# Both tiles' delta rule ahead of the norms, output rows tile by tile, and filling products in front of two norms

## The chip, the cores and the metric

The kernel runs on one core of a Trainium2 chip. The metric is the device time of one execution in microseconds, as the median of the runs.

## What is computed

Two blocks of a network run one after the other on 256 rows of width 1024, batch 1. The first is a mixer of sparse attention, pooling and a gated spatial unit, then attention to a memory, then a convolutional FFN. The second is a mixer of a gated delta rule, an indexed sparse attention and a long convolution, then cross attention to a second memory (`mem_2`), then an MLP. Each part adds its result to the rows `x` of the residual stream. What the change touches, cut from the reference:

```
x = x + rms_norm(memory_attention(h, m, w_mq, w_mk, w_mv, w_mo), mem_norm_post)
h = rms_norm(x, ffn_norm_pre)
x = x + rms_norm(conv_ffn(h, w_up, conv_w, conv_b, w_down), ffn_norm_post)
...
gamma = where(tril, exp(where(tril, decay_i - decay_j, 0)), 0)
a_mat = where(strict, (k beta) k^T * gamma, 0);  solve (I + a_mat) [u, w] = [v beta, k beta exp(decay)]
step: v_new = u - w S;  o = q exp(dec) S + (q k^T gamma) v_new
      S = S exp(last) + (k exp(last - dec))^T v_new
o = rms_norm_2(o, norm_g) * silu(z)
```

All of it is in fp32, to be matched closely.

## The kernel before

The 256 rows are two tiles of 128. A product of fp32 numbers is made of three passes of TensorE (`mm3`, L240): each operand is split in a high and a low part, and high x high, low x high and high x low are summed in PSUM. `load_w` (L213) brings a weight tile of 128 x 1024 by a DMA on SP's queue into one of four `wr` buffers; ScalarE copies it to `wh` (the high part), VectorE subtracts in two halves to make `wl`. After `give(share)` every so many tiles are subtracted on GpSimd in one piece instead (L238).

The program is written as Python generators, and the emission order with the dependences sets the order on each engine; a tile framework places the waits. `lead(main, fill, ratio)` emits `ratio` steps of a filling generator for each step of a main one, and `beside` mixes two.

Four places matter here.

- **`block1_mem` (L960)**, the memory attention. `out(n, qs, i)` adds output products of `w_mo` for half n, weight quarters qs and row tile i. At its end it loads and norms `mem_2` (`mem_T`, L343) into `m2T`, loads the last constants and three quarters of the key half of `xa_wkv`, adds the last output products and calls `residual` (L448): for tile 0, then tile 1, squares (ScalarE), scaling (L461), the power -1/2 (`rms_pow`, L293, on GpSimd, L298), and the sum into x (L467).
- **`ffn` (L1043)** begins with `norm_T` (L322): for each tile the squares, the power and the scaled rows `xh` (L340), then four 128 x 128 transposes on TensorE for each half (L317), which ScalarE (L307) and VectorE (L308) copy to high and low parts `hl`. Behind it stands `xa_k` (L1641), the key half of the second memory (48 products of 512 columns, made of m2T and `xa_wkv`), whose products TensorE takes as filling. `block2_mix` (L1170) begins in the same way with `norm_T` and the value half, `xa_v`.
- **`gdn_decay` (L1253)** makes the decay mask `gamma`: outer differences (L1289), a minimum with 0 (L1293), an exponential (L1294) and a multiplication with the upper triangle on GpSimd (L1295). The lengths of q and k follow, whose power -1/2 is `gdr_y` on GpSimd (L260). The keys `ds_kn` of the sparse attention (L1524, transposed at L1525) stand behind in VectorE's queue.
- **`gdn` (L1388)** runs the two tiles in turn. For a tile: state products (L1402, L1404, tile 1 only), the solution w (L1412), the new state (L1418, tile 0 only), the output (L1423) on VectorE (L1426 to L1429), then its norm: squares, the power `gdo_y` on GpSimd, the gate z (L1440, L1441), transposes (L1444) and their copies (L1447, L1448) into the first half of `mixT`. Filling beside it is `fill2`: the end of the sparse attention, the norm of the long convolution (`conv_norm`, L1615: statistics, `sg_v` at L1632, transposes at L1623 and L1636), the residual rows added to the banks of the output sum (`add_x`, L1229), and the products of `w_out_2` with the mixer's second half (stage 0, L406 to L408). After that come the products with the first half (stage 1).

Of the kernel before, what the change touches and what calls it, by code (L numbers as in the profile page):

```python
# [8 lines left out]
F32 = mybir.dt.float32  # L9
# [11 lines left out]
P = 128  # L21
# [25 lines left out]
_CONST = [("ident", 128), ("blk8", 8), ("blk2", 2), ("upper", 128), ("trineg", 128), ("lev", 7 * 128)]  # L47
# [79 lines left out]
class Net:  # L127
# [202 lines left out]
    def row_norm_T(self, x, g, dst, i, tag="tp"):  # L330

        nc = self.nc
        ss = self.half_sums(EPS)
# [3 lines left out]
        for n in range(2):  # L337
            sl = slice(n * 512, (n + 1) * 512)
            a = self.t([P, 512], "xh", bufs=4)
            nc.vector.scalar_tensor_tensor(a, x[:, sl], r, g[:, sl], op0=ALU.mult, op1=ALU.mult)  # L340
            self.transpose_split(a, dst, i, 4 * n, 4, tag)

    def mem_T(self, name, gname, place=None, tag="fl"):  # L343

        nc = self.nc
        g = self.grow(gname)
# [16 lines left out]
    def proj_half(self, wname, n, h, nk=NCH, tag="cc", late=False, ws=()):  # L363
# [14 lines left out]
        return a  # L378

# [68 lines left out]
    def residual(self, xs, acc, gname=None):  # L448

        nc = self.nc  # L450
        g = self.grow(gname) if gname else None
        for i in range(2):
            x = xs[i]
            if gname:
                ss = self.half_sums()
                z = []
                for n in range(2):
                    sl = slice(n * 512, (n + 1) * 512)
                    self.square_sum(acc[n][i], ss[:, n:n + 1])
                    a = self.t([P, 512], "xh", bufs=4)  # L460
                    nc.vector.scalar_tensor_tensor(a, acc[n][i], ROOT_D, g[:, sl], op0=ALU.mult, op1=ALU.mult)  # L461
                    z.append(a)
                r = self.rms_pow(ss)
            for n in range(2):
                sl = slice(n * 512, (n + 1) * 512)
                if gname:
                    nc.vector.scalar_tensor_tensor(x[:, sl], z[n], r, x[:, sl], op0=ALU.mult, op1=ALU.add)  # L467
                else:
                    nc.vector.tensor_tensor(x[:, sl], acc[n][i], x[:, sl], op=ALU.add)
        return xs  # L470

# [333 lines left out]
    def fill1(self, hT, mixT, x2):  # L805
# [9 lines left out]
        mT = self.mem_T("mem", "mem_norm_kv", "t3")  # L815
# [144 lines left out]
    def block1_mem(self, x):  # L960
# [47 lines left out]
        query(1)  # L1008
        step(first)
# [886 lines left out]
```

## Time and profile before

| | |
|---|---|
| median of three runs | 862.19 us (858.83, 862.19, 863.39) |
| the profiled execution | 860.27 us, span 858.5 us |
| mean granted clock of TensorE | 0.987 |
| TensorE busy | 829.3 us (97%) |
| VectorE, ScalarE, GpSimd busy | 623.6, 494.6, 71.0 us |

One execution was profiled. Its span runs from the first to the last instruction; 1.8 us lie around it. The busy time of TensorE counts overlapped products, so 97% says that it nearly always has something under way, and the places of interest are the few microseconds in which it has not, and the ones in which it runs at a lower granted clock (a column of the stretches).

### The profile page before, as it was taken

The page shows a single profiled execution, that of the slowest core. Times are in us where ns is not written, and L with a number is a line of the kernel's source. Part 1 is how long each engine was busy: PE and PEld are TensorE (multiplying, and loading weights), DVE is VectorE, ACT ScalarE, POOL GpSimd, SP SyncE. Part 2 cuts the span into 40 slices and gives each one's busy share as a digit, 9 for nine tenths or more (in the row PEclk, how much of TensorE's full clock was granted, in tenths as well). Part 3 has the DMA queues.
Part 4 walks back from the last instruction along what each step waited for, and adds up shares of the span by engine and source line. Part 5 has one row for each costly group of instructions (what it writes and reads, how often), then busy time and mean ns, then how long its engine had stood idle before and what let it go on. Part 6 is the DMA issues. An engine that isn't in the chain of part 4 may idle for free.

```text
span 858.5 us, 13849 instructions
## 1 busy us (share of the span) xinstructions
PE 829.3 (97%) x5117; PEld 729.5 (85%) x5117; DVE 623.6 (73%) x1394; ACT 494.6 (58%) x889; POOL 71.0 (8%) x105
## 2 busy tenths in 40 slices
PE   8899999999998999999999999999899999999998
PEld 6898877889877888888887998989798988888886
DVE  5469765554577988988886797988676876666663
ACT  6256554554665776766665764656365665555552
POOL 1224101121110000000001002000100000000000
PEclk9899999999999999999999999999999999999999
DMA  8994323464562576665642562302153366655651
GB/s 267 287 291 161 99 78 117 145 226 148 171 222 98 196 233 213 218 212 183 194 150 74 195 194 80 98 1 81 36 179 99 106 214 195 188 182 195 192 182 68
DMA packets 41007, 138.86 MB, mean 162 GB/s; under 512 B 4851, under 2 KB 6292, under 8 KB 40940
## 3 DMA queue, kind: packets, MB, share of 16 engines
q1 hardware_dynamic: 37440, 130.49, 46.6%
q10 hardware_dynamic: 2988, 6.06, 2.1%
q0 software_dynamic: 512, 1.44, 1.0%
q8 instruction: 40, 0.66, 0.3%
q14 instruction: 27, 0.22, 0.1%
HBM read 136.00 MB, written 1.44 MB: 160 GB/s over the span
## 4 chain that ended last, share of the span: by engine, by line
PE 76%; DVE 8%; DMA 7%; ACT 3%; issue 2%; POOL 2%; ACTq 0%; SPq 0%; POOLq 0%; DVEq 0%
PE tp L527 14%; PE tp L528 8%; PE fl L242 6%; PE fl L244 6%; PE fl L243 6%; PE cc L242 4%; PE cc L244 4%; PE cc L243 4%; DMA wr<-in_w_in_dram 3%; PE tp L530 2%; PE tp L242 2%; DVE wl L232 2%; PE tp L243 2%; PE tp L244 2%; PE cc L787 1%
## 5 line engine op out<-in xcount | busy, mean ns | idle before, releaser
L232 DVE TENSOR_TENSOR wl<-wr,wh 128x512 fp32r<-128x512 f32 (+2 forms) x446 | 296.8, 690 | 93.4 <-ACT wh L230 92.8
L230 ACT ACTIVATE wh<-wr 128x1024 fp32r<-128x1024 f32 (+2 forms) x223 | 231.8, 1042 | 101.0 <-PE fl L243 25.0
L527 PE MATMUL tp<-hl,wh 128*128 128x512 f32 x532 | 190.6, 397 | 0.0
L528 PE MATMUL tp<-hl,wl 128*128 128x256 f32 x608 | 158.2, 281 | 0.0
L528 PEld LDWEIGHTS tp<-hl,wl 128*128 128x128 f32 x608 | 114.7, 189 | 6.6
L527 PEld LDWEIGHTS tp<-hl,wh 128*128 128x128 f32 x532 | 100.0, 188 | 21.6
L242 PE MATMUL tp<-hl,wh 128*128 128x256 f32 x176 | 51.4, 293 | 3.5 <-ACT wh L230 3.5
L244 PE MATMUL tp<-hl,wl 128*128 128x256 f32 x176 | 51.1, 290 | 0.0
L243 PE MATMUL tp<-hl,wh 128*128 128x256 f32 x176 | 50.9, 290 | 0.0
L1062 DVE SCALAR_TENSOR_TENSOR ff_y<-ff_u,col,ff_y 128x255 f32<-128x255 f32 x88 | 41.9, 478 | 1.4 <-ACT ff_y L1060 1.2
L242 PE MATMUL fl<-hl,wh 128*128 128x256 f32 x144 | 42.1, 292 | 0.4 <-ACT sg_v L893 0.4
L242 PE MATMUL cc<-wh,ff_h 128*128 128x512 f32 x108 | 42.4, 393 | 0.0
L242 PE MATMUL fl<-wh,ff_h 128*128 128x512 f32 x108 | 42.3, 392 | 0.0
L243 PE MATMUL cc<-wl,ff_h 128*128 128x512 f32 x108 | 42.3, 392 | 0.0
L244 PE MATMUL fl<-wh,ff_h 128*128 128x512 f32 x108 | 42.3, 392 | 0.0
L244 PE MATMUL cc<-wh,ff_h 128*128 128x512 f32 x108 | 42.3, 392 | 0.0
L243 PE MATMUL fl<-wl,ff_h 128*128 128x512 f32 x108 | 42.0, 389 | 0.0
L237 ACT ACTIVATE ff_h<-ff_y 128x256 fp32r<-128x256 f32 x54 | 22.3, 416 | 33.7 <-PE fl L244 25.2
L243 PE MATMUL fl<-hl,wh 128*128 128x256 f32 x144 | 41.7, 289 | 0.0
L244 PE MATMUL fl<-hl,wl 128*128 128x256 f32 x144 | 41.6, 289 | 0.0
L242 PEld LDWEIGHTS tp<-hl,wh 128*128 128x128 f32 x176 | 35.0, 199 | 3.9 <-ACT wh L230 3.7
L531 ACT ACTIVATE ff_y<-tp 128x256 f32<-128x256 f32 x32 | 12.3, 383 | 43.8 <-PE tp L530 43.8
(504 smaller groups left out, 1952.4 us busy)
## 6 DMA issues: line engine op xcount, KB each, us to landing
wr<-in_mlp_w_dram SPq DMA_DIRECT2D x64, 512.0 KB, 3.5
wr<-in_w_up_dram SPq DMA_DIRECT2D x44, 512.0 KB, 3.7
wr<-in_w_in_dram SPq DMA_DIRECT2D x31, 512.0 KB, 4.3
wr<-in_w_down_dram SPq DMA_DIRECT2D x22, 512.0 KB, 3.4
wr<-in_w_out_dram SPq DMA_DIRECT2D x16, 512.0 KB, 3.6
grow<-in_rows_dram ACTq DMA_DIRECT2D x8, 512.0 KB, 5.2
wr<-in_w_mk_dram SPq DMA_DIRECT2D x8, 512.0 KB, 4.5
wr<-in_w_mv_dram SPq DMA_DIRECT2D x8, 512.0 KB, 3.5
```

Source lines behind the costliest of these rows:

```text
L230: nc.scalar.activation(hi, raw, AF.Copy)
L232: nc.vector.tensor_tensor(lo[:, q], raw[:, q], hi[:, q].bitcast(F32), op=ALU.subtract)
L237: nc.scalar.activation(hi, raw, AF.Copy)
L242: nc.tensor.matmul(out, a[0], b[0], start=first, stop=False)
L243: nc.tensor.matmul(out, a[0], b[1], start=False, stop=False)
L244: nc.tensor.matmul(out, a[1], b[0], start=False, stop=last)
L527: nc.tensor.matmul(pts[e], hi, both[:, :, k, :], start=k == 0, stop=False)
L528: nc.tensor.matmul(pts[e][:, :S], lo, h[0][:, k, :], start=False, stop=False)
L530: nc.tensor.matmul(pts[e], hi, both[:, :, k, :], start=False, stop=True)
L531: nc.scalar.activation(dst[:, e, :], pts[e][:, S:], AF.Copy)
L787: nc.tensor.matmul(out[:, h * 64:(h + 1) * 64], pT[:, (e * (i + 1) + b) * P:(e * (i + 1) + b + 1) * P], vsw[b][:, vo:vo + 64], start=(b == ...
L1062: nc.vector.scalar_tensor_tensor(y[:, e, k:], a[:, :S - k], self.c("conv_w", 44 * (2 - k) + c), y[:, e, k:], op0=ALU.mult, op1=ALU.add)
```

## The change

Four things are changed; the results stay the same sums.

- In `block1_mem`, `give(0)` stands behind the second query, so that no weight tile from there is subtracted on GpSimd. The two rows tiles of `mem_2` are loaded and normed ahead of the last two quarters of both output halves, and both rows of gains are loaded there. The output products of tile 0 (both halves) come first, then tile 0's part of the residual (`residual_tile`), the second memory's transposes, and then tile 1's products and residual.
- `norm_beside` puts three of the four weight quarters of the key half (`ffn`) and of the value half (`block2_mix`) in front of the norm, and the fourth behind it. `half_steps` is the generator of the quarters; `row_norm_T` is cut in `row_norm` and `rows_T`.
- In `gdn_decay` the minimum and the mask are one operation, with a constant of large negative numbers below the diagonal (`neglow`, 128 more columns of constants); the multiplication on GpSimd is left out.
- In `gdn` a first loop runs both tiles' recurrence, and a second loop both norms, with one more `yield` between a norm and its transposes.

```
@@ block1_mem
         query(1)
+        self.give(0)
         step(first)
...
-        for i in range(2):
-            out(0, (2, 3), i)
-        self.m2T = self.mem_T("mem_2", "norm_mem_2", tag="tp")
+        g2, g = [self.grow(n) for n in ("norm_mem_2", "mem_norm_post")]
+        self.m2T = self.new_T()
+        rows = [self.wp.tile([P, D], F32, tag="wr", name=self.nm("wr")) for _ in range(2)]
+        for i in range(2):
+            nc.sync.dma_start(rows[i], self.i["mem_2"][i])
+        m = self.row_norm(rows[0], g2)
+        out(0, (2, 3), 0)
+        self.rows_T(m, self.m2T, 0)
+        m = self.row_norm(rows[1], g2)
+        out(1, (2, 3), 0)
+        self.residual_tile(x[0], [a[0] for a in acc], g)
+        self.rows_T(m, self.m2T, 1)
...
-        for i in range(2):
-            out(1, (2, 3), i)
-        return self.residual(x, acc, "mem_norm_post")
+        for n in range(2):
+            out(n, (2, 3), 1)
+        self.residual_tile(x[1], [a[1] for a in acc], g)
+        return x
@@ ffn (block2_mix in the same way, with the value half)
-        hT = self.norm_T(x, "ffn_norm_pre")
-        self.xa_k()
+        acc, steps = self.half_steps("xa_wkv", 0, self.m2T, ws=self.ahead)
+        hT = self.norm_beside(x, "ffn_norm_pre", steps)
+        self.xa_k(acc)
@@ new
+    def half_steps(self, wname, n, h, tag="cc", ws=()):
+        a = [self.ps(tag) for _ in range(2)]
+        def steps():
+            for q in range(NCH // 2):
+                w = ws[q] if q < len(ws) else self.load_w(self.i[wname][n, q])
+                for i in range(2):
+                    self.part_N(a[i], h, w, i, q, NCH)
+                yield
+        return a, steps()
+    def norm_beside(self, x, gname, steps):
+        for _ in range(3):
+            next(steps)
+        hT = self.norm_T(x, gname)
+        for _ in steps:
+            pass
+        return hT
@@ gdn_decay
+        low4 = self.con[:, CON["neglow"]:CON["neglow"] + P].unsqueeze(1).to_broadcast([P, H, P])
...
-            nc.vector.tensor_scalar(gam[:, i], gam[:, i], 0.0, None, op0=ALU.min)
+            nc.vector.scalar_tensor_tensor(gam[:, i], gam[:, i], 0.0, low4, op0=ALU.min, op1=ALU.add)
             nc.scalar.activation(gam[:, i], gam[:, i], AF.Exp)
-            nc.gpsimd.tensor_tensor(gam[:, i], gam[:, i], up4, op=ALU.mult)
@@ gdn, behind the recurrence of a tile
             yield
 
+        for i in range(2):
+            tsl = slice(i * P, (i + 1) * P)
+            o = os[:, i]
             sv = self.t([P, H], "gd_sv")
...
             nc.vector.tensor_tensor(o, o, b4(ro), op=ALU.mult)
+            yield
             pt = self.ps()
```

On SP's queue the two loads of `mem_2` move from behind the sixth tile of `w_mo` to behind the fourth. At three places TensorE's order shows the change.

The first is the norm ahead of the FFN. Before, the groups of transposes of `xh` (L317) stand among the last products of the key half (`cc`, of m2T's `hl`), starting behind its first quarters:

```order
1278 L244 MATMUL cc_2805<-t_557_2659,hl_2594 128x512
1279 L317 MATMUL tp_2761<-con,xh_2759 128x128 x4
1280 L242 MATMUL cc_2805<-t_557_2659,hl_2594 128x512
1281 L317 MATMUL tp_2770<-con,xh_2768 128x128 x4
1282 L243 MATMUL cc_2805<-gd_rhs_2658,hl_2594 128x512
1283 L244 MATMUL cc_2805<-t_557_2659,hl_2594 128x512
1284 L317 MATMUL tp_2789<-con,xh_2787 128x128 x4
```

In the changed kernel they stand together behind the third quarter, and the fourth quarter (of `wh` and `wl`) follows:

```order
1287 L244 MATMUL cc_2750<-t_571_2693,hl_2560 128x512
1288 L317 MATMUL tp_2804<-con,xh_2800 128x128 x4
1289 L317 MATMUL tp_2811<-con,xh_2802 128x128 x4
1290 L317 MATMUL tp_2832<-con,xh_2828 128x128 x4
1291 L317 MATMUL tp_2839<-con,xh_2830 128x128 x4
1292 L242 MATMUL cc_2749<-wh_2848,hl_2560 128x512
```

So all four groups moved behind 36 products, and 12 products are left behind them.

The second is the end of tile 0's delta rule. Before, behind tile 0's output (L1423) come a few filling products, tile 0's transposes for its norm (L1444), and only then tile 1's state products (L1402):

```order
2982 L407 MATMUL cc_6590<-hl_4945,wh_6669 128x256
2983 L408 MATMUL cc_6590<-hl_4945,wl_6670 128x256
2984 L1444 MATMUL tp_6528<-con,t_1060_5471 128x128 x4
2985 L1402 MATMUL tp_6609<-gd_st_6499,kq_5160 128x128 x2
2986 L1636 MATMUL fl_6581<-con,sg_v_6579 128x128
```

In the changed kernel, whose line numbers are 46 to 52 higher here, the state products (L1450, L1452) follow the output (L1471) of tile 0 at once:

```order
2968 L1466 MATMUL tp_6495<-t_1060_5474,gd_kd_6369 128x128 x4
2969 L1471 MATMUL tp_6502<-t_1060_5474,bq_1106_5658 128x128 x4
2970 L1450 MATMUL tp_6516<-gd_st_6500,kq_5163 128x128 x4
2971 L1452 MATMUL tp_6517<-gd_st_6500,kq_5163 128x128 x4
2972 L1688 MATMUL fl_6568<-con,sg_v_6566 128x128
```

Tile 0's transposes moved behind tile 1's output, 19 rows further on.

The third is tile 1's transposes. Before, they stand among the products of stage 0 of `w_out_2`:

```order
3051 L407 MATMUL fl_6591<-hl_4945,wh_6720 128x256
3052 L408 MATMUL fl_6591<-hl_4945,wl_6721 128x256
3053 L1444 MATMUL tp_6711<-con,t_1060_5471 128x128 x4
3054 L406 MATMUL fl_6591<-hl_4945,wh_6720 128x256
3055 L407 MATMUL fl_6591<-hl_4945,wh_6720 128x256
```

In the changed kernel they stand behind the last of them; the next four products are one of each bank of stage 1, and the rest of stage 1 follows:

```order
3082 L440 MATMUL fl_6600<-hl_4948,wl_6733 128x256
3083 L1496 MATMUL tp_6774<-con,t_1060_5474 128x128 x4
3084 L438 MATMUL cc_6597<-hl_4948,wh_6788 128x256
3085 L438 MATMUL cc_6598<-hl_4948,wh_6825 128x256
3086 L438 MATMUL fl_6599<-hl_4948,wh_6862 128x256
3087 L438 MATMUL fl_6600<-hl_4948,wh_6899 128x256
3088 L439 MATMUL cc_6597<-hl_4948,wh_6788 128x256
```

The products of stage 0 that stood behind these transposes moved ahead of them.

## Rows read from the trace of the kernel before

**Rows 1.** TensorE's waits over the whole run: us in total, times, longest us.
```profile
PE tp L317 <- DVE xh L340: 5.9, 4, 2.7
```

**Rows 2.** Stretches of 10 us: length, busy of five engines, clock, DMA share, GB/s.
```profile
260.00:270.00 10.00, 10.00 (x48) 8.35 (x48) 5.07 (x9) 4.73 (x13) 0.60 (x2) 0.84 0.29 108
...
460.00:470.00 10.00, 9.73 (x55) 7.87 (x54) 4.84 (x10) 4.43 (x8) 0.60 (x1) 1.00 0.29 102
...
520.00:530.00 10.00, 8.17 (x66) 7.68 (x65) 6.90 (x24) 5.17 (x14) 3.54 (x4) 0.98 0.30 105
530.00:540.00 10.00, 10.00 (x72) 9.62 (x71) 7.93 (x28) 4.81 (x8) 1.46 (x1) 0.85 0.01 2
...
600.00:610.00 10.00, 6.91 (x49) 6.24 (x48) 5.49 (x13) 3.73 (x11) 1.90 (x3) 0.90 0.16 52
610.00:620.00 10.00, 10.00 (x80) 9.82 (x79) 6.42 (x12) 4.29 (x9) 1.24 (x1) 0.93 0.01 2
```

**Rows 3.** Timeline of TensorE, 249.5 to 268.5, and VectorE's `xa_kn`: start, length, then names.
```profile
249.95 0.39 PE L242 MATMUL cc<-t,hl 128*128 128x512 f32 x1
250.17 0.39 PE L243 MATMUL cc<-bq,hl 128*128 128x512 f32 x1
...
259.80 1.04 PE L317 MATMUL tp<-con,xh 128*128 128x128 f32 x4 [2.67 <-DVE xh L340]
260.49 0.78 PE L242 MATMUL cc<-t,hl 128*128 128x512 f32 x1
...
265.79 0.63 PE L317 MATMUL tp<-con,xh 128*128 128x128 f32 x4
266.17 0.48 PE L243 MATMUL cc<-wl,hl 128*128 128x512 f32 x1
...
268.10 0.39 PE L527 MATMUL tp<-hl,wh 128*128 128x512 f32 x1
...
272.42 0.69 DVE L1654 TENSOR_TENSOR xa_kn<-cc,xak_y 128x512 f32<-128x512 f32 x1
```

**Rows 4.** Timeline of GpSimd's powers and a VectorE subtraction beside the first, 254 to 261.
```profile
254.05 0.68 DVE L232 TENSOR_TENSOR wl<-wr,wh 128x512 fp32r<-128x512 f32 x1
...
254.21 0.93 POOL L298 TENSOR_TENSOR rms_y<-rms_v,mhalf 128x1 f32<-128x1 f32 x1 [2.15 <-DVE rms_v L296]
...
260.52 0.55 POOL L298 TENSOR_TENSOR rms_y<-rms_v,mhalf 128x1 f32<-128x1 f32 x1 [1.62 <-DVE rms_v L296]
```

**Rows 5.** Timeline of TensorE at the second mixer's norm, 453 to 469.
```profile
453.34 0.39 PE L242 MATMUL cc<-t,hl 128*128 128x512 f32 x1
...
459.67 0.63 PE L317 MATMUL tp<-con,xh 128*128 128x128 f32 x4 [1.04 <-DVE xh L340]
...
468.37 0.28 PE L242 MATMUL cc<-wh,hl 128*128 128x268 f32 x1
```

**Rows 6.** Timeline of VectorE, GpSimd and TensorE at the decay mask, 522 to 528.
```profile
522.24 0.41 DVE L1293 TENSOR_SCALAR t<-t 128x512 f32<-128x512 f32 x1
...
524.40 1.09 POOL L1295 TENSOR_TENSOR t<-t,con 128x512 f32<-128x512 f32 x1
525.45 1.64 POOL L260 TENSOR_TENSOR gdr_y<-gd_ss,mhalf 128x8 f32<-128x8 f32 x1
...
528.07 0.33 PE L1525 MATMUL cc<-con,ds_kn 128*128 128x128 f32 x1 [1.83 <-DVE ds_kn L1524]
```

**Rows 7.** Timeline of TensorE and ScalarE at the end of the delta rule, 606 to 623.
```profile
606.96 0.63 PE L1444 MATMUL tp<-con,t 128*128 128x128 f32 x4 [2.74 <-DVE sg_var L1629]
...
621.02 0.63 PE L1444 MATMUL tp<-con,t 128*128 128x128 f32 x4 [0.47 <-DVE t L1441]
...
621.68 0.69 ACT L1447 ACTIVATE hl<-tp,col 128x512 fp32r<-128x512 f32 x1 [1.96 <-PE tp L1444]
622.63 1.06 ACT L230 ACTIVATE wh<-wr 128x1024 fp32r<-128x1024 f32 x1 [0.26 <-PE fl L407]
```

**Rows 8.** DMA issues over the whole run: KB each, median us from issue to landing.
```profile
wr<-in_w_mo_dram SPq DMA_DIRECT2D x8, 512.0 KB, 4.6
```

More of the change, by code (lines that the diff above doesn't have):

```diff
@@ L330, in row_norm_T, with row_norm @@
     def row_norm_T(self, x, g, dst, i, tag="tp"):
+        self.rows_T(self.row_norm(x, g), dst, i, tag)
+    def row_norm(self, x, g):
         nc = self.nc
+        halves = []
         ss = self.half_sums(EPS)
@@ L340, in row_norm_T, with rows_T, mem_T @@
             nc.vector.scalar_tensor_tensor(a, x[:, sl], r, g[:, sl], op0=ALU.mult, op1=ALU.mult)
+            halves.append(a)
+        return halves
+    def rows_T(self, halves, dst, i, tag="tp"):
+        for n, a in enumerate(halves):
             self.transpose_split(a, dst, i, 4 * n, 4, tag)
-    def mem_T(self, name, gname, place=None, tag="fl"):
+    def mem_T(self, name, g, place=None, tag="fl"):
         nc = self.nc
-        g = self.grow(gname)
         dst = self.new_T(place)
@@ L448, in residual, with residual_tile @@
     def residual(self, xs, acc, gname=None):
-        nc = self.nc
         g = self.grow(gname) if gname else None
         for i in range(2):
[L453 to L469, printed above, removed]
-        return xs
+            self.residual_tile(xs[i], [a[i] for a in acc], g)
+        return xs
+    def residual_tile(self, x, acc, g):
+        nc = self.nc
+        halves = slice(0, 512), slice(512, 1024)
+        if g is None:
+            for n, sl in enumerate(halves):
+                nc.vector.tensor_tensor(x[:, sl], acc[n], x[:, sl], op=ALU.add)
+            return
+        ss = self.half_sums()
+        z = []
+        for n, sl in enumerate(halves):
+            self.square_sum(acc[n], ss[:, n:n + 1])
+            a = self.t([P, 512], "xh", bufs=4)
+            nc.vector.scalar_tensor_tensor(a, acc[n], ROOT_D, g[:, sl], op0=ALU.mult, op1=ALU.mult)
+            z.append(a)
+        r = self.rms_pow(ss)
+        for n, sl in enumerate(halves):
+            nc.vector.scalar_tensor_tensor(x[:, sl], z[n], r, x[:, sl], op0=ALU.mult, op1=ALU.add)
     def build_bias(self):
@@ L1172, in block2_mix @@
         W = "w_in_2"
-        hT = self.norm_T(x, "norm_mix_2")
-        self.xa_v()
+        acc, steps = self.half_steps("xa_wkv", 1, self.m2T, ws=self.ahead)
+        hT = self.norm_beside(x, "norm_mix_2", steps)
+        for i in range(2):
+            nc.scalar.activation(self.kv2[1][i], acc[i], AF.Copy)
         mixT = self.new_T()
@@ L1774, in _constants @@
     put("trineg", np.where(r[:, None] >= r[None, :], 0, NEG).astype(f))
+    put("neglow", np.where(r[:, None] <= r[None, :], 0, NEG).astype(f))
     lev = np.zeros((P, 7, P), f)
```

10 lines of the change are left out of this document (3 added, 7 removed).

## The prediction

> **What bounds the kernel now.** I read first who TensorE waits for, summed over the run, then what the clock does in stretches of 10 us, and last the timeline of each place where the two agree. TensorE is the engine that sets the end nearly everywhere, so a microsecond is won only where it stands idle or runs at its lower level. The list of waits is led by a line that the change touches, 5.9 us in four waits on the transposes of the norms (L317, held by VectorE's `xh`; the longest 2.7) [rows 1]. The timelines show two more: 2.74 us at the transposes behind the delta rule (L1444) [rows 7], and 1.83 at the keys of the sparse attention (L1525, beside `gdn_decay`) [rows 6]. The stretches [rows 2] show what each gap costs beyond itself. Behind the gaps of 2.67, 1.83 and 2.74 us the granted clock is 0.84, 0.85, and 0.90 with 0.93; since a product takes 0.78 instead of 0.39 there [rows 3], that is time at 1.2 GHz in place of 2.4: 10 x (1 - 0.84) = 1.6 us of work lost behind the first, 1.5 + 0.2 behind the second, 1.0 + 0.7 behind the third, less where TensorE idled anyway. A gap of 1.04 us [rows 5] left 460 to 470 at 1.00 [rows 2]. So a gap brought near one microsecond gives back its clock too.
>
> **Part 1, the norm ahead of the FFN.** From the first product of the key half (249.95) to the first product of `w_up` (268.10) pass 18.15 us [rows 3]. They hold 48 products, one every 0.22 to 0.23 us (249.95 to 250.17), so 10.9 us, and four groups of transposes at 0.38 (265.79 to the next product at 266.17), 1.5 us: 12.4 us of work and 5.7 lost. Before, `residual` takes both tiles behind the last output product, and the norm's last half reaches TensorE at 265.79, 15.8 us after 249.95. After, tile 0's output products, its residual and half of that chain lie ahead of tile 1's products, under TensorE's own work. I halve 15.8 to 7.9 and add 2 to 2.5 us for tile 0's norm, which shares VectorE with tile 1 (operations of 0.68 and powers of 0.55 to 0.93 [rows 4]): the last `xh` is there at 259.9 to 260.4. TensorE has 36 products first (to 258.1), then tile 0's transposes (0.8, to 258.9), waits 1.0 to 1.5, does tile 1's (0.8) and 12 products (2.7): `w_up` starts at 263.4 to 263.9, a gain of 4.4 of the 5.7. From it I take 0.8: `xa_kn` came at 272.42 + 0.69, 5.0 us behind the start of `w_up` at 268.10 [rows 3], and the new order puts the key transposes behind some 4 us of `w_up` products. I enter **3.5**, bounds 2.0 (the whole tile 0 norm in the way, and 1.1 at the keys) and 4.8 (no wait at the norm, none at the keys).
>
> The power on GpSimd took 0.93 us at 254.21, while VectorE had a subtraction of two SBUF tensors from 254.05 to 254.73, and 0.55 at 260.52 beside none [rows 4]. The Trainium skill, "SBUF — State Buffer", Who interferes with whom, says that such an operation and a GpSimd operation that reads SBUF lock one another out for a whole instruction. By this rule each of the three powers that remain in tile 1's chain and tile 0's norm could be 0.4 later, since the change puts more splits on VectorE, and the gain of this part would be 2.4 in place of 3.5; the rows agree with the rule, and my lower bound lies under its figure.
>
> What part 1 moves besides: `give(0)` sends three weight splits from GpSimd to VectorE, each two halves of 0.68 [rows 4], 4.1 us in a stretch where TensorE is never without work; VectorE has idle time there, so nothing on the path. The two `mem_2` rows go onto SP's queue ahead of the last four `w_mo` tiles and hold two of the four `wr` buffers; ScalarE's squares of those rows stand in its queue ahead of the splits of these tiles. A `w_mo` load lands 4.6 us after its issue [rows 8]; the four tiles are wanted some 20 us later, so I enter 0, with 1 us as the bound (the last tile's split arrives as TensorE asks for it), and the case in which that cover is gone is rival C. Both rows of gains are loaded ahead on ScalarE's queue: nothing waits for them.
>
> **Part 2, the norm ahead of the second mixer.** The same three pieces of 12 products stand in front of the transposes. From 453.34 to 468.37 are 15.03 us [rows 5]; 48 products and the transposes are again 12.4, so 2.6 are lost, of which 1.04 is the gap at 459.67. There is no half-clock here. 36 products end at 453.34 + 8.2 + the first 0.2 of waiting = 461.8, and VectorE's last `xh` was ready only a little after that; what stays is some 0.9 us. I enter **1.7**, bounds 1.0 and 2.4.
>
> **Part 3, the mask in `gdn_decay`.** The DVE minimum of 0.41 [rows 6] becomes an operation with a second tensor; the nearest row for that is the 0.68 of [rows 4], so + 0.27, twice. The two multiplications L1295 on GpSimd go. The second stood from 524.40 to 525.49 just ahead of the power `gdr_y` (525.45, 1.64), for which VectorE, and behind it `ds_kn` and TensorE until 528.07, waited [rows 6]. `gdr_y` comes 1.05 earlier, and the order has five more filling products ahead of the waiting transposes (0.12 each, 0.6 us): the gap of 1.83 shrinks to 0.2 to 0.4. That is 1.4, and with the gap the lower clock behind it: 1.3 of the 1.7. For VectorE, which is nearly full ahead of this, I take off 0.5. I enter **2.2**, bounds 0.5 (the clock falls all the same, VectorE is later by 0.54 and more) and 3.0.
>
> **Part 4, both tiles' recurrence ahead of the norms.** TensorE stood still for 2.74 us at 606.96 for the first tile's norm and 0.47 at 621.02 for the second's [rows 7], 0.27 lies between, and the clock cost 1.0 + 0.7 [rows 2]. In the new order tile 1's state products follow tile 0's at once (order in front), so the 2.74 is filled with work, and its clock comes back: 3.5 + some 1.3. New waits take some of it. First, `sg_v` now stands on VectorE behind tile 1's output sum, so the next transposes of the convolution branch's norm (L1688 of the changed file) wait about 0.8. Second, tile 1's transposes now stand behind all products of the first half of `w_out_2`: ScalarE must split the last weight there (1.06, it waits for the buffer of TensorE's last weight) before it copies the transposes (0.69) [rows 7], and VectorE's low half follows; only four products cover it. That is 1.06 + 0.69 + 0.7 less 0.6 of transposes and 0.5 of products, 1.4 us. I enter 4.8 - 0.8 - 1.4 = 2.6, and **2.3** for the chance that 1.4 draws the clock down; bounds 0 and 3.7.
>
> `lead` gives `gdn` 2.5 filling steps for each of its six steps now, fifteen where four steps had ten; that is why the products are spent earlier. Ahead of this, at the triangular inverse (540 to 600), the order differs by a few products and gives each level about the cover it had: 0, with 1 us either way.
>
> **The sum.** 3.5 + 1.7 + 2.2 + 0 + 2.3 = 9.7 us, against the profiled execution: 860.27 - 9.7 = 850.6. That execution is 1.9 under the median of 862.19 and 1.2 under the mean of the three runs, 861.46; I add 1.2: **851.8 us**. The bounds add to gains of 13.9 + 1 and 3.5 - 2; not all fall on one side, so I take 2.7 and 14.9; with the 1.2 these are 858.8 and 846.6, outward 859.0 and 846.0.
>
> **Rivals.** A, only half arrives: the gaps shrink but the clock still falls once, and a half of the terms comes back as waits of the neighbours (keys 1.1, `sg_v` 0.8, tile 1's evacuation at 1.4 with its clock 1.0). 9.7 / 2 = 4.9: 856.6. For it: three of the four new waits are at places with no second supply of products. Against: the two largest gaps have a full replacement in the order.
> B, the waits change their place: everything won ahead is lost at the next dependence, as the work between stays on VectorE (it does nothing less than before, and 4.1 + 0.5 us more). Gain 0 to 3, 860. For it: VectorE, not TensorE, ends the chain at each of the four gaps. Against: TensorE is full between these places, so time won on it stays won.
> C, slower: the early `mem_2` rows. If their buffers come free only after the row's norm, the last two `w_mo` tiles are issued that much later. A missing buffer costs one round of landing and splitting, 4.6 + 1.06 + 1.36 = 7.0 us, two 14.0: 850.6 + 14.0 + 1.2 = 865.8. It decides the sign once TensorE waits over 9.7 us ahead of the last output products. For it: four buffers and a strict queue. Against: the tiles are needed some 20 us after the earliest issue.
> D, the change doesn't do what it says, because the planner's order keeps the old places: the order of the changed file rules it out, under 1 in 100.
>
> **How the numbers follow.** The forecast has 0.62, A 0.18, B 0.14, C 0.05, D 0.01. The range 846.0 to 859.0 holds the forecast with its bounds and A. A measurement tells some 0.5% from no change, 4.3 us, so faster means under 857.9: the forecast nearly whole and most of A, 0.77; the same: B and the rest of A, 0.18; slower: C and what it shares with B, 0.05.
>
> **What the profile after would show.** Part 1: no L317 wait above 1.5 us near 259, clock 1.00 from 260 on, `w_up` 4 us after its place now, counted from the first key product (13.5 in place of 18.15). Part 2: 13.3 in place of 15.03. Part 3: no gap over 0.5 at `ds_kn`, clock 1.00 behind it. Part 4: no wait near 2.7, but a new one of 1 to 1.5 us behind the second tile's transposes (L1499, L1500). Wrong it would be if TensorE waits at `w_mo`, if the clock falls behind the new gap, or if the middle of the triangular inverse has new gaps.

## The result and the profile after

The changed kernel takes 849.71 us in the median of four runs (847.61 to 854.57); the kernel before, run beside it and counted with the three runs shown ahead, 861.12. The medians differ by 11.4 us; the ratio estimated from the runs is 0.9882 with a 95% interval of 0.9848 to 0.9917, so 10.2 us less (7.1 to 13.1). Forecast were 851.8 us and 9.7 us less. The profiled execution of the changed kernel took 848.02 us with a span of 846.2, 12.25 us less than the profiled one of before.

TensorE's waits over the whole run of the changed kernel (us in total, times, longest us); lines behind the new helpers have numbers up to 52 higher than before (L340 is L345, L1444 is L1496), the helpers at L230 to L317 keep theirs:

```profile
PE tp L317 <- DVE xh L345: 2.4, 2, 2.0
PE tp L242 <- ACT wh L230: 2.2, 1, 2.2
...
PE cc L438 <- ACT hl L1499: 1.2, 1, 1.2
...
PE tp L1496 <- DVE t L1492: 0.9, 1, 0.9
```

The line on L317, 5.9 us in [rows 1], is down to 2.4, of which 2.0 belong to a norm in the first block that the change leaves alone. The waits of 2.74 [rows 7] and 1.83 [rows 6] are gone. L1499 and L1492 are new.

The stretches that answer to [rows 2], in columns as there. They lie 4 to 13 us earlier in the program now:

```profile
250.00:260.00 10.00, 9.54 (x49) 7.81 (x48) 8.39 (x17) 4.62 (x12) 2.41 (x6) 1.00 0.77 256
260.00:270.00 10.00, 9.90 (x57) 8.17 (x55) 8.21 (x30) 6.27 (x23) 0.00 (x0) 1.00 0.34 112
...
520.00:530.00 10.00, 9.51 (x77) 9.00 (x76) 8.82 (x32) 4.32 (x7) 1.64 (x1) 1.00 0.01 2
530.00:540.00 10.00, 10.00 (x87) 9.95 (x86) 10.00 (x35) 5.14 (x8) 0.00 (x0) 1.00 0.33 107
590.00:600.00 10.00, 8.78 (x72) 8.02 (x71) 7.82 (x18) 4.30 (x11) 2.17 (x3) 1.00 0.31 98
600.00:610.00 10.00, 10.00 (x82) 9.63 (x82) 5.68 (x11) 4.56 (x10) 1.01 (x1) 1.00 0.14 41
610.00:620.00 10.00, 8.76 (x71) 8.32 (x71) 6.26 (x11) 4.20 (x7) 0.00 (x0) 1.00 0.54 171
```

The clock is 1.00 in all of them, and TensorE's idle time is under 0.5 us in the first four and 1.2 us in each of the two stretches of the delta rule's end. The gaps themselves, in the timeline of TensorE of the changed kernel (start, length, names, idle before and its releaser); the first row of the norm, the first of `w_up` (to [rows 3]), the gap at `ds_kn` (to [rows 6]), and three at the delta rule (to [rows 7]):

```profile
259.75 1.29 PE L317 MATMUL tp<-con,xh 128*128 128x128 f32 x8 [0.46 <-DVE xh L345]
...
263.65 0.39 PE L561 MATMUL tp<-hl,wh 128*128 128x512 f32 x1
...
520.98 0.33 PE L1577 MATMUL cc<-con,ds_kn 128*128 128x128 f32 x1 [0.18 <-DVE ds_kn L1576]
...
598.38 0.63 PE L1496 MATMUL tp<-con,t 128*128 128x128 f32 x4 [0.89 <-DVE t L1492]
599.34 0.33 PE L1688 MATMUL fl<-con,sg_v 128*128 128x128 f32 x1 [0.33 <-DVE sg_v L1684]
...
612.79 0.51 PE L438 MATMUL cc<-hl,wh 128*128 128x256 f32 x2 [1.17 <-ACT hl L1499]
```

The whole difference can be laid out along TensorE's own landmarks. The fourth column is the same stretch in those experiments below whose code is the old one there, one execution each:

| stretch of TensorE | before | changed | old code elsewhere | forecast gain, measured gain |
|---|---|---|---|---|
| first attention probabilities (L946) to first key product | 43.24 | 43.28 | 43.23 to 43.74 | 0, 0 |
| first key product to `w_up` | 18.15 | 13.58 | 16.16 to 18.58 | 3.5 with the keys, 4.57 |
| `w_up` to first value product | 185.24 | 185.37 | 185.15 to 185.25 | in the line above, -0.13 |
| first value product to the decay mask (L1275) | 55.76 | 54.03 | 55.75 to 55.82 | 1.7, 1.73 |
| the decay mask to the delta rule's first product (L1412) | 89.30 | 84.75 | 88.42 to 90.85 | 2.2 + 0, 4.55 |
| from there to the sums behind the output product (L443) | 45.10 | 43.38 | 43.97 to 45.15 | 2.3, 1.72 |
| to the last product | 210.61 | 210.66 | 210.62 to 210.65 | 0, 0 |

So the sum came out near: 12.3 us between the two profiled executions and 10.2 by the ratio, against 9.7, with one term too small by 2.4 and two off by 0.6 to 1.1. That 9.7 lies so close to 10.2 is in part luck, since by the stretches the terms miss by 2.6 in all.

The fourth column says why the last is to be read with care. The longer times in it belong to executions in which the granted clock fell behind a gap. Where the old code ran with the clock at 1.00, the three stretches of parts 1, 3 and 4 took 16.16, 88.42 and 43.97 to 44.01 us. Against these single executions the change is worth 2.6, 3.7 and 0.6; the other 2.0, 0.9 and 1.1 us are stretches at the lower clock in the profiled execution of before.

### The profile page after: what moved, and what is told of

Read it like the earlier page. It is cut to its first block, busy times and chain, and to the rows that moved or that the text cites. A ratio compares the mean times of both kernels' runs of the same rounds, so it can differ in the third digit from the quotient of the medians.

```text
span 846.2 us, 13853 instructions
## 1 busy us (share of the span) xinstructions
PE 825.2 (98%) x5117; PEld 726.5 (86%) x5117; DVE 628.6 (74%) x1400; ACT 494.0 (58%) x889; POOL 62.8 (7%) x100
## 4 chain that ended last, share of the span: by engine, by line
PE 78%; DVE 10%; ACT 4%; DMA 4%; POOL 2%; issue 2%; ACTq 0%; SPq 0%; POOLq 0%; DVEq 0%
PE tp L561 14%; PE tp L562 8%; PE fl L242 6%; PE fl L244 6%; PE fl L243 6%; PE cc L242 5%; PE cc L244 5%; PE cc L243 5%; PE tp L242 2%; PE tp L244 2%; DVE wl L232 2%; PE tp L243 2%; PE tp L564 2%; DMA wr<-in_w_in_dram 2%; PE cc L821 1%
## 5 line engine op out<-in xcount | busy, mean ns | idle before, releaser
L232 DVE TENSOR_TENSOR wl<-wr,wh 128x512 fp32r<-128x512 f32 (+2 forms) x452 | 301.0, 691 | 82.6 <-ACT wh L230 81.5
L230 ACT ACTIVATE wh<-wr 128x1024 fp32r<-128x1024 f32 (+2 forms) x226 | 234.9, 1042 | 99.3 <-PE fl L243 21.1
L561 PEld LDWEIGHTS tp<-hl,wh 128*128 128x128 f32 x532 | 100.0, 188 | 21.6
L242 PE MATMUL tp<-hl,wh 128*128 128x256 f32 x176 | 50.9, 290 | 2.2 <-ACT wh L230 2.2
L242 PE MATMUL fl<-hl,wh 128*128 128x256 f32 x144 | 42.3, 293 | 0.7 <-ACT wh L230 0.6
L242 PE MATMUL cc<-wh,ff_h 128*128 128x512 f32 x108 | 42.4, 393 | 0.0
L242 PE MATMUL fl<-wh,ff_h 128*128 128x512 f32 x108 | 42.3, 392 | 0.0
L565 ACT ACTIVATE ff_u<-tp 128x256 f32<-128x256 f32 x44 | 16.9, 385 | 37.0 <-PE tp L564 36.7
L565 ACT ACTIVATE ff_y<-tp 128x256 f32<-128x256 f32 x32 | 12.3, 383 | 43.8 <-PE tp L564 43.8
```

What stands on the lines that cost most here:

```text
L230: nc.scalar.activation(hi, raw, AF.Copy)
L232: nc.vector.tensor_tensor(lo[:, q], raw[:, q], hi[:, q].bitcast(F32), op=ALU.subtract)
L242: nc.tensor.matmul(out, a[0], b[0], start=first, stop=False)
L561: nc.tensor.matmul(pts[e], hi, both[:, :, k, :], start=k == 0, stop=False)
L565: nc.scalar.activation(dst[:, e, :], pts[e][:, S:], AF.Copy)
```

## The experiments

Each part was put alone into the kernel before, then parts were divided, and two versions of the end of the delta rule and one of the weight splits were tried on the changed kernel. Ratios are to the kernel before in the same series. The ratios of the four parts alone fall short of 1 by 0.44, 0.15, 0.58 and 0.01%, together 1.18%, which is what the changed kernel has; each of them is uncertain by some 0.2%.

**The mask alone.** The diff is that of `gdn_decay` in the part on the change.

> The kernel before with the mask as part of the minimum, and nothing else changed. The changed kernel gained 4.5 us between the first outer difference of the decay mask and the delta rule's first product, of which I had forecast 2.2 for the mask and 0 for the triangular inverse. Theory: all of it comes from the mask, since gdr_y is earlier and nothing else of the change lies there: no wait at ds_kn over 0.3 us, clock 1.00 from 530 to 540, 4.5 us less in that stretch, 855.8 us against 860.3. Rival: only the gap and its clock come from the mask, 2.2 to 3.0 us, and the rest at the triangular inverse from the new order of gdn's filling: 857.3 to 858.1, with idle time of about 1.7 us left from 550 to 590.

Ratio 0.9956 (0.9932 to 0.9981); the profiled execution 852.75 us. The stretch from the decay mask to the delta rule took 84.98 us, and the wait at `ds_kn` 0.19: nearly the whole gain (4.32 of 4.55) comes with the mask alone. The first theory holds for the place of the gain; the rival's 1.7 us of idle time in the triangular inverse are not there (0.7 us from its first step to the delta rule). But 852.75 is less than either expected, because unchanged places were faster too, and that became the main finding. The timeline and the stretches of this kernel, whose norm ahead of the FFN and whose delta rule are those of before (columns as above):

```profile
258.81 0.63 PE L317 MATMUL tp<-con,xh 128*128 128x128 f32 x4 [2.62 <-DVE xh L345]
...
600.51 0.63 PE L1481 MATMUL tp<-con,t 128*128 128x128 f32 x4 [2.75 <-DVE sg_var L1666]
```

```profile
250.00:260.00 10.00, 7.38 (x38) 5.92 (x37) 8.44 (x17) 5.07 (x12) 2.94 (x7) 1.00 0.53 167
260.00:270.00 10.00, 9.57 (x52) 7.62 (x51) 7.20 (x24) 5.65 (x21) 0.14 (x2) 1.00 0.25 97
600.00:610.00 10.00, 9.22 (x74) 8.62 (x75) 5.84 (x11) 3.65 (x7) 0.56 (x1) 1.00 0.01 2
610.00:620.00 10.00, 9.53 (x81) 9.36 (x80) 7.18 (x14) 4.59 (x9) 1.39 (x1) 1.00 0.47 137
```

Both gaps stand there at their old length, 2.62 and 2.75 us, and the clock stays at 1.00 behind both. The stretch from the first key product to `w_up` took 16.16 us instead of 18.15 with the same instructions (18.18 in the kernel with the mask as two operations, which has the same order of TensorE there).

**The delta rule alone.** The diff is that of `gdn`.

> The kernel before with both tiles' recurrence ahead of the norms, nothing else changed. Theory: the gain lies behind the delta rule's first product only, 1.7 us as in the changed kernel: no wait of 2.7, but one of 0.9 at tile 0's transposes and one of 1.2 behind tile 1's; 858.6 us. Rival (the order reaches back into the triangular inverse): 2 us more ahead of it, 856.5, with less idle time from 550 to 590 than the 1.7 us of before.

Ratio 0.9985 (0.9964 to 1.0006). The stretch behind the delta rule's first product took 43.42 us, with waits of 0.89, 0.33 and 1.17 at the places of the changed kernel; the stretch ahead of it 89.28, as before. The theory holds, and this part has nothing to do with the triangular inverse.

**The first place alone, with both its halves.**

> The kernel before with all of the first place: no splits on GpSimd behind the second query, the second memory's rows ahead, output rows tile by tile, and three pieces ahead of the FFN's norm; the second mixer, the mask and the delta rule as before. Theory: 4.4 us from the first key product to the first product of w_up, and the same offset to the end: 855.9. Rival (it is given back by the keys or in the FFN): under 3 us, above 857.3.

Ratio 0.9942 (0.9923 to 0.9961). 13.58 us from the first key product to `w_up`, to the hundredth what the changed kernel has, and the offset stays to the end: as the theory said.

**The second mixer's norm alone.**

> The kernel before with three pieces ahead of the second mixer's norm, nothing else changed. Theory: 1.7 us between the first value product and the first product of w_in_2, no wait at L317 over 0.3 there; 858.6. Rival (the gain depends on the earlier start of the row chain, or is given back in the projections): under 0.7 us, above 859.6.

54.02 us for the stretch, 1.74 less, and no wait at L317 there: the theory holds. The ratio is 0.9999 (0.9979 to 1.0019): the median does not show 1.7 us, since the scatter of single runs is larger (855.93 to 862.65).

**The rows of the first place without the pieces.** In this family of kernels `norm_beside` takes the number of pieces ahead as its last argument. The FFN's norm gets none (cut from the edit; the second mixer, the mask and the delta rule are as before, and `give(0)` is left out):

```diff
-        hT = self.norm_beside(x, "ffn_norm_pre", steps)
+        hT = self.norm_beside(x, "ffn_norm_pre", steps, 0)
```

> The kernel before with the first place's rows alone: no GpSimd splits behind the second query, the second memory's rows ahead, output rows tile by tile; no pieces ahead of the FFN's norm. From the first key product to the first product of w_up: 18.15 us before, 13.58 with both halves of the change. Theory (the chain of squares, power and scaled rows is what ends there, and taking tile 0 out of it is the gain): tile 0's transposes stand behind 27 products and wait about 1 us for xh, tile 1's come at the same time as in the changed kernel, so 14.5 to 15, a gain of 3.2 to 3.7 of the 4.57. Rival (it is the pieces ahead that fill the gap): over 16.5, and a wait of 2 us or more is left.

14.73 us: a gain of 3.42 against the profiled execution of before, with a wait of 1.19 at tile 0's transposes and one of 0.44 at tile 1's. The theory holds for the waits. This kernel kept the weight splits on GpSimd, other than its expectation says; what that did stands with the last two experiments.

**The pieces without the rows.** Three pieces ahead of the FFN's norm, `block1_mem` as before.

> The kernel before with three pieces ahead of the FFN's norm alone; the output rows and the second memory as before. Same stretch. Theory (the row chain ends there): the last xh comes as late as before, some 12.5 us behind the first key product, so a wait of 1.5 us or more stays at the first transposes and one at tile 1's; 16 us, a gain of about 2. Rival (the pieces are the gain): 14.5 or less.

15.75 us, a gain of 2.40, with waits of 0.38, 0.62 and 0.92. The theory's size holds, its waits are smaller and three. The two halves give 3.42 and 2.40 alone and 4.57 together, which looks as if each filled a part of the same gap. But the clock stayed at 1.00 in this stretch in both halves, and fell in the execution of before, so its 2.0 us are counted in each of the three. Against the old code with the clock at 1.00 (16.16) the rows are worth 1.43 alone, the pieces 0.41, and both 2.58: the pieces are worth little until the rows end the chain earlier, which is what the theory said of the chain.

**The mask as two operations on VectorE.**

```diff
             nc.scalar.activation(gam[:, i], gam[:, i], AF.Exp)
-            nc.gpsimd.tensor_tensor(gam[:, i], gam[:, i], up4, op=ALU.mult)
+            nc.vector.tensor_tensor(gam[:, i], gam[:, i], up4, op=ALU.mult)
```

> The kernel before with the mask's multiplication moved from GpSimd to VectorE as an operation of its own (0.68 us, twice), the minimum kept: VectorE has 0.4 us more for each tile than with the joined operation, GpSimd is as free. From the first outer difference to the delta rule's first product: 89.30 before, 84.98 with the joined operation. Theory (GpSimd's queue ahead of gdr_y is the gain): within 0.5 us of 84.98, no wait at ds_kn over 0.5. Rival (VectorE, full there, sets the end): 85.8 or more.

88.01 us: the theory falls, and the rival's 85.8 or more holds, though it named no size. Up to the first step of the triangular inverse the theory does hold: 28.84 us against 28.16 with the joined operation and 30.70 before, and the wait at `ds_kn` is 0.27. So the freed GpSimd is what closes that gap. Behind it, to the delta rule, the kernel takes 59.17 us, against 56.82 with the joined operation and 58.60 before. A new wait stands there, in TensorE's timeline of this kernel:

```profile
567.37 0.66 PE L1504 MATMUL tp<-con,t 128*128 128x128 f32 x4 [1.29 <-DVE t L1523]
```

Two masks with the same GpSimd queue thus differ by 2.35 us in the triangular inverse, where the order of TensorE and VectorE came out different. That VectorE's extra work holds it up there isn't excluded. What this says of the 2 us is weighed below.

**The delta rule with fewer filling steps.** In the changed kernel:

```diff
-        lead(self.gdn(kq, z, mixT), fill, R2)
+        lead(self.gdn(kq, z, mixT), fill, 1.75)
```

> The changed kernel with 1.75 filling steps for each step of the delta rule in place of 2.5: tile 1's transposes stand ahead of 75 products of the first half of w_out_2 and not behind them, so the 1.17 us for the split and the copy behind them is covered. Theory: those transposes now come too early; their rows are ready about 6.7 us behind tile 1's output, TensorE is there after 3.5, and waits about 3: 1.8 us slower than the changed kernel from the delta rule's first product on (43.38 us to the end of the output sum there), 45 or more, with the clock down behind the wait in some executions. Rival (the copy is the only cost): 42.2, and 1.2 us faster than the changed kernel.

43.95 us, between the two, and neither is right. The wait behind the copy is gone and so is any wait at tile 1's transposes, since TensorE was held up ahead of them. TensorE's and VectorE's timeline of this kernel:

```profile
597.96 0.74 DVE L1500 SCALAR_TENSOR_TENSOR hl<-tp,col,hl 128x512 fp32r<-128x512 f32 x1
598.78 0.54 DVE L1684 TENSOR_SCALAR sg_v<-fl,sg_mv,rms_y 128x256 f32<-128x256 f32 x1
...
599.38 0.33 PE L1688 MATMUL fl<-con,sg_v 128*128 128x128 f32 x1 [2.33 <-DVE sg_v L1684]
```

```profile
600.00:610.00 10.00, 10.00 (x72) 9.81 (x71) 4.14 (x9) 3.28 (x6) 1.02 (x1) 0.83 0.07 16
```

The other ratio also moved `sg_v` on VectorE behind tile 0's low half (L1500), and its product waits 2.33 us where it waited 0.33. Behind that wait the granted clock falls (0.83 from 600 to 610, the stretch above, columns as before), so the 43.95 us hold some time at the lower clock as well. The median was 847.87, ratio 0.9858 (0.9827 to 0.9888), not to be told from the changed kernel.

**The same aim without moving the rest.** The last bank's filling step is cut in two, and the steps are dealt out by hand:

```diff
-                if c % 2:
+                if c % 2 or (st == 0 and j == 8 // per - 1):
                     yield (j * per + c) // 2
...
-        lead(self.gdn(kq, z, mixT), fill, R2)
+        for n, _ in zip((2, 3, 2, 2, 0, 0), self.gdn(kq, z, mixT)):
+            for _ in range(n):
+                next(fill, None)
```

> The changed kernel with its last filling step cut in two and its steps dealt out as 2, 3, 2, 2, 0, rest: up to the norms the order is that of the changed kernel, and 12 products of the first half of w_out_2 stand behind tile 1's transposes, with ScalarE's copy of them ahead of the split of the last weight. Theory (the wait of 1.17 is the split ahead of the copy, with no products left to cover it): no wait of over 0.3 us behind tile 1's transposes, from the delta rule's first product to the end of the output sum 42.2 us against 43.38, nothing else moved. Rival (the split of the last weight then comes too late for its own products): a new wait of 0.7 to 1.2 at that weight, 43.0 or more. In the median 1.2 us is at the edge of what can be told.

42.08 us against 43.38, with a wait of 0.19 left of the 1.17, and nothing else moved: the theory holds. ScalarE's timeline shows the swap, first in the changed kernel, then in this one:

```profile
611.10 1.06 ACT L230 ACTIVATE wh<-wr 128x1024 fp32r<-128x1024 f32 x1 [0.98 <-PE fl L439]
612.07 0.67 ACT L1499 ACTIVATE hl<-tp,col 128x512 fp32r<-128x512 f32 x1
```

```profile
612.42 0.69 ACT L1501 ACTIVATE hl<-tp,col 128x512 fp32r<-128x512 f32 x1
613.74 1.06 ACT L230 ACTIVATE wh<-wr 128x1024 fp32r<-128x1024 f32 x1 [0.63 <-PE fl L439]
```

Before the swap the copy stands behind the split, which waits for TensorE's last weight; after it the copy goes first. The median is 845.81, ratio 0.9835 (0.9809 to 0.9861), the lowest of all versions. The changed kernel had 849.19 in the same series; 1.3 of these 3.4 us are seen in the stretches, the rest is scatter as far as the profiles tell.

**The changed kernel once more.**

> The changed kernel once more, unchanged, for a second profile and a longer series. Theory (where a gap ends up at the lower clock differs from one execution to the next, the gaps themselves don't): waits at the same places and of the same length within 0.05 us, the stretches of lower clock elsewhere or of another length, 847 to 855 us. Rival (the clock follows the program): the same stretches at the same clock as in the first profile, 30 to 50 and 170 to 190.

849.19 in the median, 852.04 for the profiled execution, 4.02 more than the first. From the first key product to the last product they differ by 0.11 us (591.77 and 591.66), and every wait there is the same within 0.02. The difference lies wholly ahead of the attention's probabilities: 206.79 and 210.94. The theory holds for the clock, and for the waits behind that point; ahead of it the waits differ too. TensorE's wait for an early weight was 2.2 us in the first execution (L242, in the list of the result) and 3.5 in this one:

```profile
PE tp L242 <- ACT wh L230: 3.5, 1, 3.5
```

The stretches, first of the first execution, then of this one:

```profile
30.00:40.00 10.00, 8.39 (x55) 8.16 (x56) 5.22 (x10) 3.81 (x6) 1.43 (x2) 0.83 1.04 316
40.00:50.00 10.00, 9.37 (x64) 9.15 (x63) 6.97 (x7) 3.20 (x5) 6.52 (x11) 0.83 1.02 252
60.00:70.00 10.00, 9.92 (x84) 9.79 (x84) 7.88 (x24) 7.34 (x17) 1.23 (x4) 1.00 0.73 246
```

```profile
30.00:40.00 10.00, 7.44 (x49) 7.22 (x50) 4.54 (x9) 3.39 (x5) 1.90 (x3) 0.83 0.98 267
40.00:50.00 10.00, 9.09 (x58) 8.87 (x58) 6.96 (x8) 3.31 (x4) 5.38 (x10) 0.80 1.02 256
60.00:70.00 10.00, 10.00 (x75) 10.00 (x75) 7.29 (x19) 6.46 (x12) 0.63 (x2) 0.83 0.66 218
```

The same program is at 1.00 in one and 0.83 in the other between 60 and 70. All waits of TensorE up to the probabilities sum to 10.3 and 11.4 us, and the clock is at its lower level for 10 and 17 us there: some 1.1 of the 4.15 us are waits, and the rest goes with the clock.

**The splits left on GpSimd, and the rows with the splits on VectorE.** The first is the changed kernel without `give(0)`, the second the rows-only kernel with it.

```diff
         query(1)
-        self.give(0)
         step(first)
```

> The changed kernel with give(0) left out: the weight splits behind the second query that GpSimd had before stay on GpSimd, 2.4 us each. Theory (those splits are off the path, as I entered them): the first product of the key half starts within 0.3 us of the changed kernel's, counted from the attention's products, and the stretch to w_up is 13.6 within 0.3. Rival (a subtraction on GpSimd locks VectorE's operations of two tensors out, as the doubled split at 244.42 of before suggests, and holds a product): a wait on wl from GpSimd, 0.3 to 1.5 us more in 240 to 265.

> The kernel of e5_rows_only with give(0) behind the second query as well (e5_rows_only itself kept those splits on GpSimd, other than its expectation says). Theory: a GpSimd split holds its buffer 1.1 us longer than VectorE's two halves, the first row of mem_2 is issued that much later, and ScalarE waits for it with the splits and copies queued behind; on VectorE the wait of ScalarE at the row's squares falls from 1.8 to under 0.5 us and the stretch from the attention's probabilities to the first key product from 44.28 to 43.3. From there to w_up 14.7 as in e5_rows_only. Rival (the second memory's rows ahead cost that wherever the split is made): 44.0 or more.

In the first, the stretch to `w_up` is 13.55 as expected, but from the probabilities to the first key product pass 44.71 us in place of 43.28: 1.43 more, so the theory falls there; it is the rival's size at another place and by another way. SP's waits from 195 to 225 and ScalarE's timeline, first in the changed kernel, then in that one (L1068 and L1067 are the loads of the `mem_2` rows):

```profile
SPq L1068 <- DVE wl L232: 8.5, 2, 6.0
SPq L1067 <- POOL wl L238: 7.2, 1, 7.2
```

```profile
210.04 0.63 ACT L279 ACTIVATE junk<-wr 128x512 bf16<-128x512 f32 x1 [0.23 <-DMA wr<-in_mem_dram]
213.49 0.63 ACT L279 ACTIVATE junk<-wr 128x512 bf16<-128x512 f32 x1 [2.29 <-DMA wr<-in_mem_dram]
```

GpSimd takes 2.38 us for a split and holds the `wr` buffer for all of it; VectorE's halves take 1.29. SP's load of the first `mem_2` row waits for that buffer, 7.2 us in place of 6.0, and ScalarE then stands 2.29 us at the row's squares (0.23 in the changed kernel) with the next split and copies behind it. In the rows-only kernel the wait is 1.84 and the stretch 44.28 us; with `give(0)` it is 0.36 and 43.27, as the last theory said. So the two edits belong together: the early rows without `give(0)` cost 1.0 to 1.4 us, and `give(0)` takes that away.

## Why the prediction was right, and where it was not

**Part 1** was entered at 3.5 and gave 4.57. Its chain was sized well: the transposes of tile 1 came at 259.75 (forecast 259.9 to 260.4), `w_up` 13.58 us behind the first key product (13.5). TensorE waited 0.46 there, where 1.0 to 1.5 were forecast. The 0.8 taken off for the keys was wrong: the stretch behind `w_up` grew by 0.13 only. That single executions of the old code needed 16.16 to 18.58 means that 2.6 to 5.0 us would have been right, by how the clock fell: with it at 1.00 on both sides, 2.6.

**Part 2** was entered at 1.7 and gave 1.73, and 1.7 to 1.8 in every pair of kernels. No clock had a hand in it.

**Part 3** was entered at 2.2 with 0 for the triangular inverse, and gave 4.55; this is the mis-sized term. Cut at the first step of the inverse (L1478 of before), the two halves tell more. Ahead of it the time fell from 30.70 to 28.21, so 2.5 against the 2.2: the gap shrank by 1.65 (1.83 to 0.18, forecast 0.2 to 0.4), `gdr_y` came 1.05 earlier as worked out, a new wait of 0.30 (L1518) takes some back, and the clock gave the rest. The clock was entered at 1.3. The old code took 29.56 us there in the one execution with the clock up, some 30.7 in four and 32.25 in two, so it costs 0 to 2.7.

The step that failed is "the order gives each level about the cover it had: 0", with its 1 us either way. From the first step of the inverse to the delta rule the time fell from 58.60 to 56.54 in the changed kernel, to 56.82 with the mask alone, and rose to 59.17 with the mask as two operations. The granted clock was 1.00 there in every execution, so it is not the clock. Before, TensorE waits four times there, 0.2 to 0.8 us, and I left these out as small; in the changed kernel one of them is left, at `bq`. In TensorE's timeline, first before, then the changed kernel:

```profile
559.30 0.61 PE L1327 MATMUL fl<-ones,gd_sq 128*128 128x1 f32 x4 [0.22 <-ACT gd_sq L1324]
567.74 2.05 PE L1484 MATMUL tp<-t 128*128 128x128 f32 x16 [0.79 <-ACT t L1479]
576.80 0.66 PE L1466 MATMUL tp<-con,t 128*128 128x128 f32 x4 [0.34 <-DVE t L1485]
582.84 0.39 PE L242 MATMUL fl<-wh,hl 128*128 128x256 f32 x1 [0.36 <-DVE bq L1376]
```

```profile
572.06 0.39 PE L242 MATMUL fl<-wh,hl 128*128 128x256 f32 x1 [0.49 <-DVE bq L1424]
```

The waits give 1.2 of the 2.1 us, and two of TensorE's 460 operations now lie ahead of the inverse. All executions with the old mask have the same order of TensorE, VectorE and ScalarE from the decay mask to the delta rule and took 58.60 to 58.88 us for the inverse; the changed kernel and the mask alone share another order (56.5 to 56.8), the two operations have a third. So the runs tie these levels to the order, 2.1 us less or 0.6 more. Which moved product does it, or whether it is VectorE's lead as the inverse begins, stays open; no run took that apart.

**Part 4** was entered at 2.3 and gave 1.72 against the profiled execution of before, and 0.6 to 1.8 against the eight executions with the old code: 0.6 against the three with the clock at 1.00, 1.5 to 1.8 against the five in which it fell. The mechanism was right at each point named: the gap of 2.74 filled, a wait at `sg_v` (0.33, forecast 0.8), a wait of 1.17 behind the copy of tile 1 (forecast 1.4), for the reason given, the split ahead of the copy. One wait was overlooked, 0.89 at tile 0's transposes, held by `t` behind the power on GpSimd. And the term for the clock, 1.3, was paid in five of eight executions.

The claim "a gap brought near one microsecond gives back its clock too" held for the changed kernel (1.17 and 0.89, clock 1.00 in both executions). From 130 us on it holds in every trace: gaps of 0.88 to 1.29 us stand there some fifty times, and the clock fell behind none. Ahead of that it doesn't: from 40 to 50 us the changed kernel is at 0.83 (stretches above), with no wait longer than 0.63 us in the ten before it fell. Its other half, that the gaps of 1.83 and of 2.67 to 2.74 cost the clock, is a matter of chance in a single execution. The clock fell behind 4 of 5 gaps at the FFN's norm, 6 of 7 at `ds_kn` and 5 of 8 at the end of the delta rule; with the mask alone two of them stood, and the clock stayed up. The plainest case is a norm in the first block which no experiment touches: the same gap of 1.94 to 1.96 us stands in all fourteen traces, and the clock fell behind it in seven. The gap and the stretch behind it, in the changed kernel, where the clock fell, and with the mask alone, where it didn't:

```profile
177.31 0.66 PE L317 MATMUL tp<-con,xh 128*128 128x128 f32 x4 [1.95 <-DVE xh L345]
180.00:190.00 10.00, 10.00 (x62) 8.91 (x61) 5.65 (x10) 4.44 (x7) 3.15 (x3) 0.91 0.59 211
```

```profile
178.00 0.66 PE L317 MATMUL tp<-con,xh 128*128 128x128 f32 x4 [1.94 <-DVE xh L345]
180.00:190.00 10.00, 9.69 (x63) 8.34 (x62) 6.09 (x11) 4.99 (x8) 3.38 (x3) 1.00 0.64 215
```

What a profile shows behind a gap is one draw; I took it for the price.

The rule of the Trainium skill that the prediction weighed ("SBUF — State Buffer", Who interferes with whom) is borne out again: in the changed kernel the norm's powers took 0.86, 0.86 and 0.55 us, the long ones while VectorE subtracts two SBUF tensors (L232, from 251.79 to 252.47 and from 255.51 to 256.20), in GpSimd's timeline there:

```profile
252.02 0.86 POOL L298 TENSOR_TENSOR rms_y<-rms_v,mhalf 128x1 f32<-128x1 f32 x1 [5.82 <-ACT wh L230]
...
255.75 0.86 POOL L298 TENSOR_TENSOR rms_y<-rms_v,mhalf 128x1 f32<-128x1 f32 x1 [2.82 <-DVE rms_v L296]
...
258.27 0.55 POOL L298 TENSOR_TENSOR rms_y<-rms_v,mhalf 128x1 f32<-128x1 f32 x1 [1.61 <-DVE rms_v L296]
```

The 2.4 that the prediction worked out by that rule for part 1 is not borne out: two of three powers took 0.3 us longer, and the part still gave 4.57. The chain of before, which the estimate halves, had two such powers already, 0.93 us [rows 4] and this one:

```profile
258.00 0.86 POOL L298 TENSOR_TENSOR rms_y<-rms_v,mhalf 128x1 f32<-128x1 f32 x1 [2.82 <-DVE rms_v L296]
```

Rival C's mechanism exists at no price: in the changed kernel SP waits 6.6 us, in two waits, for `xh` of the `mem_2` rows before it loads the next `w_mo` tiles, and no product waits for them. What did cost is a relative of it, the 2.29 us that ScalarE waits for the `mem_2` row when the splits stay on GpSimd. Its price was 1.43 us and not 14, and the change itself took it away with `give(0)`, which I had entered as neutral. A and B did not come about: what was won at each place stayed won to the end (table).

## What to carry to other kernels

Behind the start of the program, take a gap's length from the profile as the same in every execution, but not the lower clock behind it: look at the same stretch in several executions, and enter the clock as a range from zero. Compare two kernels by executions that have the same clock in the stretch, or the gains of two halves will hold the same microseconds twice. Where a wait is removed ahead of a stretch whose second engine is nearly full (VectorE was busy for 54 of the inverse's 58.6 us), the order behind it changes too; put a bound of a few per cent of that stretch on it (here 2.1 of 58.6). And two edits that look independent, a load moved ahead and a split moved to another engine, can share one buffer: ask who holds the buffer that the early load needs.

## What the runs showed of the hardware

- The start of this program, up to the memory attention's probabilities, took from 202.59 to 210.94 us in fourteen executions whose code is the same there but for one split. The fastest is the one in which the granted clock never fell to 1.2 GHz there, the slowest the one in which it stood there longest (17 us); between them the clock orders them only in part, and TensorE's waits differ too (9.2 to 12.3 us in sum). The rest of the changed kernel repeated within 0.11 us. That the scatter of its runs, 847 to 855, is mostly this was seen for the two that were profiled.
- The same gap was followed by the lower clock in some executions and not in others: 7 of 14 at 1.95 us, 6 of 7 at 1.83, 9 of 13 at 2.6 to 3.0. The stretch behind it took up to 2.7 us more or nothing. Behind gaps of 0.88 to 1.29 us, from 130 us on, it was followed in none of some fifty.
- A GpSimd subtraction beside a VectorE one of two SBUF tensors: VectorE's two halves, begun at 242.00, took 2.64 us instead of 1.29, while GpSimd's ran from 241.10 to 243.49 (the changed kernel without `give(0)`).
